# A hybrid decoder trunk in fp32: from orders written by hand to an order planned by a list scheduler

## The chip, the core and the metric

The kernel runs on one core of one Trainium2 chip. A core has TensorE (PE in the profile; PEld are its weight loads), VectorE (DVE), ScalarE (ACT), GpSimd (POOL), and SyncE (SP), whose queue issues most of the transfers. Each engine takes its instructions strictly in the order in which they are written, and waits by semaphores for what other engines or transfers have to finish first. The metric is the time of one execution in microseconds (us) on the device; of several runs the median counts.

## What is computed

Two layers of a decoder over 256 tokens with a width of 1024. A layer has a token mixer of three branches that read one projection of the normalized input, then cross-attention to 256 memory tokens, then a SwiGLU feed-forward part with an inner width of 2816.

```
for l in range(DEPTH):                                     # 2
    h = rmsnorm(x, norm_gains[l, 0])
    y = hybrid_mixer(h, ...)
    x = x + rmsnorm(y, norm_gains[l, 1])
    h = rmsnorm(x, norm_gains[l, 2]);  m = rmsnorm(mem, mem_norm[l])
    x = x + rmsnorm(cross_attention(h, m, ...), norm_gains[l, 3])
    h = rmsnorm(x, norm_gains[l, 4])
    x = x + rmsnorm(swiglu_ffn(h, ...), norm_gains[l, 5])

def hybrid_mixer(h, w_in, ...):
    z = h @ w_in
    z_q, z_kv, z_ng, z_rwkv, z_s5, z_mg = split(z)
    y_nsa  = nsa_attention(...)          # sparse attention, 8 heads of 64
    y_rwkv = rwkv7_time_mix(z_rwkv, ...) # recurrence over the tokens, 4 heads
    y_s5   = s5_layer(z_s5, ...)         # diagonal state space, 16 groups
    g_nsa, g_rwkv, g_s5 = split(sigmoid(z_mg))
    merged = g_nsa * (y_nsa @ w_up_nsa) + g_rwkv * (y_rwkv @ w_up_rwkv) + g_s5 * (y_s5 @ w_up_s5)
    return merged @ w_out
```

## The kernel before

**The main stream.** All large weights come in units of 128 x 1024 numbers, 135 a layer. SP loads a unit into `raw` (three buffers). ACT copies it, rounded, into the high part `wh` (L298), and DVE or POOL subtracts that from `raw` to get the low part `wl` (L299); of `wh` and `wl` there are four buffers each. This is called a split below. A product of two fp32 matrices is then three matmuls with these parts (`mm3`, L349 to L351): high by high, high by low, low by high. "Product" below means one of these single matmuls; a layer has 2688, and they are counted from the start of the run. In the order of the first layer: 1 to 48 the queries (512 columns wide), 49 to 288 the inputs of the RWKV and S5 branches (256 wide), 289 to 384 keys and values (48 of them 512 wide, 48 of them 280 wide), 385 to 864 most of the gates (256 wide), then to 1152 the up-projections of the three branches and the last gates, then the output projection, cross-attention and the feed-forward part.

**The small steps.** The branches RWKV (`rwkv`, stream r), S5 (`s5`, s) and sparse attention (`nsa`, n) have hundreds of small matmuls, DVE steps, ACT steps and POOL steps each. `drive` writes one step of a stream at a time, in the order of a string of letters, `MIX`, one for each layer, with m for the main stream (`mixer_main`). `XA_STEPS` does the same for cross-attention. The up-projections need the results of the branches (`yr`, `y5`, `yn`).

**What sets the order.** The order in which the code writes the instructions, moved a little by the framework's own scheduler, which knows a raised priority for a few functions (the decorator `@first`, and `HPX`): `NormT.tile`, `Post.half`, `Post.end`. The engine of each split comes from short lists, `ENGS`, which `W.engs = engs(n)` puts into force from a place on. `Weights.ahead` writes a split up to three units ahead of its products. PSUM has eight banks: three go round among the main stream's sums (`mm`), five among all else (`px`).

**Norms.** `NormT` transposes the input by token tiles (two of 128 tokens, `x` for each), splits it in high and low parts (L416 on ACT, L417 on DVE), and works out the reciprocal root of the mean square (`stat`, `rsqrt`, L366 to L381 on DVE, eight small steps in a chain), which `row` spreads along a row. `Post` scales a sub-layer's result and adds it to `x` (L444 to L458), with the same chain of small steps.

**S5 parameters.** `s5_params` makes tables from the parameters of S5 with some 170 small POOL instructions a layer on tiles of 128 x 8 (`tiny`, helpers at L465 to L500). POOL also carries splits, in the same queue.

Of the kernel before, what the change touches and what calls it, by code (L numbers as in the profile page):

```python
# [17 lines left out]
L = 2  # L18
# [9 lines left out]
# the order in which the steps of streams are written  # L28
XA_STEPS = 'kkEQ00Fv101vv0Ov1010110'
MIX = ['rmsrnmnsmrrsrmrnsmnrssnmmssmrmrrmrsnrsnnsmsnnsmrnssrmrrnmnmrsnrsnmrsnmrsrrmnmrsnmmrsnsnnrnmsmmrsnmrnrsnsmsrnrsnrmnssnrrmnsrmmssmrsssssrrmsmrsnsssnmnrrsmmsnnmsrrrrrsnrrrnmrnmnrsnmssssmrmnssnmmrnnssnnmmmsnmrrnnrmrsmsrmrsrsrsnnmsmssnnrnsnnrrmr', 'smsnmrmnrrmrssnnssmrsmmrsnsssrsrnmmrnnmrsmrnnrsnmmrsmmnmrsnrnrsnsmnrrrsmmnsmssnsrmnsnrrssnrnrsmrsnnmmnrsrmnmmrsnsrmmrrsnrrrssrmsnmsrnmmnnmsmnrrnsmnmnsnsmrsrmnrnnsrsrrnnnmmsnrsnrnnsnmsnmmmnsmrsmnsnrnnnrnrrrmnnmmsssrrrrsnmssnmmsrmrnmm']  # L30
# [5 lines left out]
TAIL = 2  # last units of weights, which have buffers of their own  # L36
MM = 3  # PSUM banks of the main stream
# [8 lines left out]
# ---------------------------------------------------------------- host layouts  # L46
# [81 lines left out]
def _mats(v):  # L128
    out = []
    for l in range(L):  # L130
# [39 lines left out]
U = 1024  # elements a partition in a unit of weights  # L170
# [61 lines left out]
# ---------------------------------------------------------------- the kernel  # L232

def body(tc, t):
    nc = tc.nc
    V, A, G, PE = nc.vector, nc.scalar, nc.gpsimd, nc.tensor

    def first(f):
        """instructions of f go before earlier ones that are ready, too"""
        def g(*a):  # L240
            with tc.high_priority(offset=HPX):
                return f(*a)
        return g

    ctx = ExitStack()
    const = ctx.enter_context(tc.tile_pool(name="const", bufs=1))
    wp = ctx.enter_context(tc.tile_pool(name="wp", bufs=2))
# [9 lines left out]
    def sb(shape, dt=F, tag=None, bufs=None):  # L257
# [9 lines left out]
        return ap.tile(list(shape), dt, tag=tag, name=nm(tag), bufs=bufs or 1)  # L267

    def ps(shape=(P, 512), tag="px", bufs=8 - MM, dt=F):
        return pp.tile(list(shape), dt, tag=tag, name=nm(tag), bufs=bufs)  # L270
# [11 lines left out]
    nc.scalar.dma_start(ident, t["consts"][:, 0:P])  # L282
# [3 lines left out]
    nc.sync.dma_start(xt[0], t["x"][0:P])  # L286
# [9 lines left out]
    # ---- weights: hi and lo parts that a product of one pass each carries  # L296
# [4 lines left out]
    class Weights:  # L301
        """the units in the order of use; loads and splits run ahead of the products"""

        def __init__(self, order):
            self.todo = order  # (layer, unit, elements)
            self.raw = []
            self.ready = []
            self.n = self.m = 0
            self.engs = [V]  # that split, in turn

        def load(self, d):
# [1334 lines left out]
```

## Time and profile before

| | before |
|---|---|
| median of 3 runs | 1130.83 us (1120.78 to 1131.45) |
| span of the profiled execution | 1125.9 us |
| granted TensorE clock, mean | 0.963 |
| PE busy, share of the span | 1037.2 us, 92% |
| DVE busy | 763.2 us, 68% |
| POOL busy | 647.3 us, 57% |
| ACT busy | 540.1 us, 48% |
| moved by DMA | 161.52 MB, 143 GB/s |

The profiled execution's own time is its span, 1125.9 us; the median of the timed runs lies 4.9 us above it. PE's busy time is a poor measure of how full it is, since matmuls overlap in its pipeline and their ends are modelled. Whether a stretch is full is seen from the number of matmuls in it.

### The profile page before, as it was taken

The page shows a single profiled execution, that of the slowest core. Times are in us where ns is not written, and L with a number is a line of the kernel's source. Part 1 is how long each engine was busy: PE and PEld are TensorE (multiplying, and loading weights), DVE is VectorE, ACT ScalarE, POOL GpSimd, SP SyncE. Part 2 cuts the span into 40 slices and gives each one's busy share as a digit, 9 for nine tenths or more (in the row PEclk, how much of TensorE's full clock was granted, in tenths as well). Part 3 has the DMA queues.
Part 4 walks back from the last instruction along what each step waited for, and adds up shares of the span by engine and source line. Part 5 has one row for each costly group of instructions (what it writes and reads, how often), then busy time and mean ns, then how long its engine had stood idle before and what let it go on. Part 6 is the DMA issues. An engine that isn't in the chain of part 4 may idle for free. (4 is left out here: it accounts for less than half of the span.)

```text
span 1125.9 us, 20473 instructions
## 1 busy us (share of the span) xinstructions
PE 1037.2 (92%) x7890; PEld 900.0 (80%) x7890; DVE 763.2 (68%) x1405; ACT 540.1 (48%) x1040; POOL 647.3 (57%) x762
## 2 busy tenths in 40 slices
PE   8887898999987999999888899999999869999997
PEld 7876676788875799998667776889788748999985
DVE  6667699898766646575458698796995764333633
ACT  7523244456555634454345242545565546444542
POOL 6999787533462586910147578964335434655543
PEclk9998999999988999999989899999899889999999
DMA  6530632244541446555434236223245314655552
GB/s 233 205 122 20 224 115 76 76 155 166 180 141 57 152 159 219 186 185 189 142 100 147 67 113 225 76 93 111 84 164 189 130 56 149 203 183 184 181 192 89
DMA packets 43153, 161.52 MB, mean 143 GB/s; under 512 B 5040, under 2 KB 5168, under 8 KB 41776
## 3 DMA queue, kind: packets, MB, share of 16 engines
q1 hardware_dynamic: 41472, 155.45, 40.7%
q10 hardware_dynamic: 1584, 4.77, 1.2%
q8 instruction: 62, 1.02, 0.4%
q14 instruction: 35, 0.29, 0.1%
HBM read 159.15 MB, written 1.05 MB: 142 GB/s over the span
## 5 line engine op out<-in xcount | busy, mean ns | idle before, releaser
L299 POOL TENSOR_TENSOR wl<-raw,wh 128x1024 fp32r<-128x1024 f32 (+1 forms) x123 | 296.7, 2420 | 327.4 <-ACT wh L298 322.0
L298 ACT ACTIVATE wh<-raw 128x1024 fp32r<-128x1024 f32 (+1 forms) x268 | 282.0, 1055 | 254.5 <-PE mm L350 107.4
L349 PE MATMUL mm<-b,wh 128*128 128x256 f32 x1344 | 386.7, 288 | 2.6 <-DVE b L1274 1.3
L351 PE MATMUL mm<-b,wl 128*128 128x256 f32 x1344 | 386.0, 288 | 1.0 <-DVE wl L299 1.0
L350 PE MATMUL mm<-b,wh 128*128 128x256 f32 x1344 | 384.4, 286 | 0.2 <-DVE b L945 0.2
L299 DVE TENSOR_TENSOR wl<-raw,wh 128x1024 fp32r<-128x1024 f32 (+1 forms) x145 | 196.7, 1357 | 166.8 <-ACT wh L298 166.6
L349 PEld LDWEIGHTS mm<-b,wh 128*128 128x128 f32 x1344 | 256.8, 191 | 12.0 <-issue 4.0
L351 PEld LDWEIGHTS mm<-b,wl 128*128 128x128 f32 x1344 | 256.6, 191 | 9.0 <-issue 6.7
L350 PEld LDWEIGHTS mm<-b,wh 128*128 128x128 f32 x1344 | 256.9, 191 | 5.7 <-issue 4.7
L350 PE MATMUL px<-wl,b 128*128 128x512 f32 x248 | 98.0, 399 | 0.0
L349 PE MATMUL px<-wh,b 128*128 128x512 f32 x248 | 97.0, 401 | 1.0 <-ACT b L298 1.0
L351 PE MATMUL px<-wh,b 128*128 128x512 f32 x248 | 97.2, 400 | 0.0
L349 PE MATMUL mm<-wh,b 128*128 128x512 f32 (+2 forms) x192 | 71.8, 382 | 13.0 <-ACT b L416 8.8
L351 PE MATMUL mm<-wh,b 128*128 128x512 f32 (+2 forms) x192 | 68.5, 370 | 5.5 <-DVE b L417 4.7
L350 PE MATMUL mm<-wl,b 128*128 128x512 f32 (+2 forms) x192 | 68.9, 364 | 0.5 <-DVE wl L299 0.5
L294 PE MATMUL px<-ident,b 128*128 128x128 f32 (+2 forms) x280 | 47.3, 287 | 12.8 <-DVE b L1432 6.7
L349 PEld LDWEIGHTS mm<-wh,b 128*128 128x128 f32 x192 | 39.8, 209 | 22.2 <-ACT b L416 13.4
L349 PEld LDWEIGHTS px<-wh,b 128*128 128x128 f32 x248 | 47.3, 191 | 11.9 <-ACT b L298 1.4
L351 PEld LDWEIGHTS px<-wh,b 128*128 128x128 f32 x248 | 47.1, 190 | 11.2
L350 PEld LDWEIGHTS px<-wl,b 128*128 128x128 f32 x248 | 47.2, 190 | 11.0
L416 ACT ACTIVATE b<-px,cols 128x128 fp32r<-128x128 f32 x128 | 41.1, 366 | 30.1 <-DVE b L417 17.2
L1568 POOL TENSOR_TENSOR b<-b,b 128x256 f32<-128x256 f32 x40 | 39.5, 989 | 26.8 <-ACT b L1567 26.7
(348 smaller groups left out, 1735.7 us busy)
## 6 DMA issues: line engine op xcount, KB each, us to landing
raw<-in_w SPq DMA_DIRECT2D x264, 512.0 KB, 3.5
b<-in_w SPq DMA_DIRECT2D x8, 1024.0 KB, 5.2
b<-in_gains ACTq DMA_DIRECT2D x6, 512.0 KB, 4.1
raw<-in_w SPq DMA_DIRECT2D x6, 420.0 KB, 3.1
b<-in_mem SPq DMA_DIRECT2D x4, 512.0 KB, 5.0
mats<-in_mats SPq DMA_DIRECT2D x1, 1152.0 KB, 7.6
mats<-in_mats ACTq DMA_DIRECT2D x1, 1152.0 KB, 6.8
x<-in_x SPq DMA_DIRECT2D x2, 512.0 KB, 5.3
```

The lines of the kernel that those rows point to most:

```text
L294: PE.transpose(out, in_, ident[:k, :k])
L298: A.activation(dst_h, src, AF.Copy)
L299: eng.tensor_tensor(dst_l, src, dst_h.bitcast(F), op=OP.subtract)
L349: PE.matmul(out, lh, rh, start=start, stop=False)
L350: PE.matmul(out, lh, rl, start=False, stop=False)
L351: PE.matmul(out, ll, rh, start=False, stop=stop)
L416: A.activation(self.h[:, n, sl], pt[:, kk], AF.Copy, scale=g[:, n:n + 1])
L1568: G.tensor_tensor(s_, s_, tg[:, 1], op=OP.mult)
```

## The change

The body is no longer written as it is run through. `Eng` stands for each engine and only notes every call in a list (`Rec.ops`), with the stream that it belongs to; each of the products of `mm3` is marked as part of one chain. `analyse` works out from the tiles which instruction needs which. `plan` then places the instructions, engine by engine, in the time of a model: of those that are ready, the one with the longest remaining path goes first. The durations come from a table in the kernel (`_cost`). The chain keeps its recorded order; other PE instructions are offered 150 ns late (`MARGIN`); streams may not run more than 30 places ahead of their oldest open step where nothing holds them (`NEAR`). `plan` picks the PSUM bank of every tile, within the three and five banks as before, and DVE or POOL for every split, whichever comes free for it first. The result is written as it is planned, with the framework's scheduler switched off. `ENGS`, the raised priorities and the run-ahead of `Weights` are without effect or gone. One letter of the first `MIX` stands four places earlier; the 2 MB of weights of the compression (`w1`, L1092) come in four loads of 512 KB for each of keys and values, not two of 1 MB; and the last steps of a layer (`finish`) are recorded ahead of the next layer's first weights.

```diff
+PE_LAT = 172
+MARGIN = 150
+DMA_LAT, DMA_NS = 1800, 0.0042
+W_SLOTS = {"raw": 3, "wh": 4, "wl": 4}
+NEAR = 30
+HORIZON = 60000.0
...
+def _cost(op, eng, out, ins, psum):
...
+    if eng == "V":
+        fast = what in ("tensor_scalar", "tensor_copy") and not inp and n >= 512
+        t = n / (1.92 if fast else 0.96) + 70
+        return t, t + 85
...
+    t = n * (2.28 if what != "tensor_scalar" else 1.7) + 100
...
+def plan(rec, info=None):
...
+    lvl = [0.0] * n
+    for i in range(n - 1, -1, -1):
+        occ, lat = min(info[i]["costs"].values())
...
+        b = occ
+        for j, kind in succ[i] + extra.get(i, []):
+            b = max(b, lvl[j] + ((lat + SEM) if kind else occ) * al)
+        lvl[i] = b
...
+    def offer(i, r):
+        for e in ops[i][0]:
+            rr = r + (MARGIN if e == "PE" and not ops[i][5] else 0)
+            heapq.heappush(pend[e], (rr, i))
+            heapq.heappush(ev, (max(rr, free[e]), e))
...
         def get(self):
-            self.ahead(1)
-            w = self.ready.pop(0)
-            self.ahead(AHEAD + max(0, min(TAIL, self.m + TAIL - len(self.todo))))
-            self.load(RAWS)
-            return w
+            l, u, k = self.todo[self.n]
+            self.n += 1
+            was, rec.stream = rec.stream, "w"
+            raw = sb([P, U], F, "raw", W_SLOTS["raw"])
+            SP.dma_start(raw[:, :k], t["w"][l, u, :, :k])
+            h, lo = sb([P, U], R, "wh", W_SLOTS["wh"]), sb([P, U], R, "wl", W_SLOTS["wl"])
+            rec.either = ("A",)
+            A.activation(h[:, :k], raw[:, :k], AF.Copy)
+            rec.either = ("V", "G")
+            V.tensor_tensor(lo[:, :k], raw[:, :k], h[:, :k].bitcast(F), op=OP.subtract)
...
     def mm3(out, lh, ll, rh, rl, start, stop):
+        rec.chain = True
         PE.matmul(out, lh, rh, start=start, stop=False)
         PE.matmul(out, lh, rl, start=False, stop=False)
         PE.matmul(out, ll, rh, start=False, stop=stop)
+        rec.chain = False
...
-        @first
         def tile(self, i, x):
...
+    with tc.manual_schedule():
+        for i, e in planned[0]:
+            _, what, a, k, _, _ = rec.ops[i]
+            getattr(real[e], what)(*a, **k)
```

In the changed kernel every instruction is written by the last line of this loop, L1988, and all PSUM tiles are called `bank`. PE and ACT have as many instructions as before; 41 splits go from DVE to POOL, so that 165 of 270 run there, where 124 did.

**The start, ACT's queue.** The place is the first norm and the first split; `x_81` and `x_82` are the token tiles of before, `x_74` and `x_75` those of the changed kernel, `b_9_95` and `b_5_79` the transposed high parts, `row_118` the row of both tiles' roots. Before:

```order
ACT_TABLE_LOAD
ACTIVATE b_35_166,tiny_165<-x_81 128x1024
ACTIVATE wh_97<-raw_88 128x1024
ACTIVATE b_9_95<-px_139,cols_85 128x128
ACTIVATE b_9_95<-px_152,cols_85 128x128
```

The changed kernel:

```order
ACT_TABLE_LOAD
ACTIVATE wh_82<-raw_81 128x1024
ACTIVATE wh_85<-raw_84 128x1024
ACTIVATE b_20_94,tiny_93<-x_74 128x1024
ACTIVATE wh_88<-raw_87 128x1024
ACTIVATE b_30_104,tiny_103<-x_75 128x1024
ACTIVATE row_118<-bank_70 128x256
ACTIVATE b_5_79<-bank_68,cols_77 128x128
```

The first transposed part, which the first product needs, stood right behind the first tile and the first split, and now stands behind both tiles and the row. In SP's queue the two tiles are loaded first and fourth before, and third and fifth now.

**POOL's queue in the first layer.** The place is the first split that POOL has among the inputs of the branches; the `tiny` tiles around it belong to the S5 parameters, `CC` is a table of theirs. Before, `wl_440` is the unit:

```order
TENSOR_TENSOR tiny_419<-tiny_416,tiny_398 128x8
TENSOR_SCALAR tiny_422<-tiny_390 128x8
TENSOR_SCALAR tiny_419<-tiny_419 128x8
TENSOR_SCALAR tiny_422<-tiny_422 128x8
TENSOR_TENSOR tiny_423<-tiny_390,tiny_422 128x8
TENSOR_TENSOR wl_440<-raw_131,wh_439 128x1024
TENSOR_SCALAR tiny_422<-tiny_422 128x8
TENSOR_SCALAR tiny_423<-tiny_423 128x8
```

The changed kernel, where `wl_249` is the eleventh unit of the run:

```order
TENSOR_TENSOR tiny_204<-tiny_204,tiny_202 128x8
TENSOR_TENSOR tiny_205<-tiny_205,tiny_202 128x8
TENSOR_TENSOR CC_221<-mats_78,tiny_204 128x256
TENSOR_TENSOR b_148_222<-mats_78,tiny_205 128x256
TENSOR_TENSOR b_149_223<-mats_78,tiny_204 128x256
TENSOR_TENSOR CC_221<-CC_221,b_148_222 128x256
TENSOR_TENSOR b_193_267<-b_41_115,cst 128x512
TENSOR_TENSOR b_148_222<-mats_78,tiny_205 128x256
TENSOR_TENSOR wl_249<-raw_247,wh_248 128x1024
```

Before, the split stood in the middle of the S5 parameters; now it stands behind nearly all of them, as POOL's 159th instruction: ahead of it are 145 that touch `tiny`, 3 splits and 10 others. Its first product is the 228th.

**PE's queue among the branches of the first layer.** The rows with 64x32, 32x256 and 128x256 x2 are small matmuls of RWKV (L677, L687), sparse attention and S5. Before, `wh_1518` and `wh_1619` are units of the gates:

```order
MATMUL mm_1816<-b_9_95,wh_1518 128x256
MATMUL mm_1816<-b_10_96,wh_1518 128x256
MATMUL mm_1816<-b_9_95,wl_1519 128x256
MATMUL px_1473<-b_350_1487,b_347_1477 32x256 x8
MATMUL px_1544<-b_225_927,b_222_906 64x32 x16
MATMUL px_1566<-b_66_300,mats_87 128x256
MATMUL px_1567<-b_66_300,mats_87 128x256
MATMUL px_1566<-b_66_300,mats_87 128x256
MATMUL px_1567<-b_66_300,mats_87 128x256
MATMUL mm_1971<-b_9_95,wh_1619 128x256
MATMUL mm_1971<-b_10_96,wh_1619 128x256
MATMUL mm_1971<-b_9_95,wl_1620 128x256
```

The changed kernel, behind product 864, the last that needs no branch:

```order
MATMUL bank_68<-b_189_263,b_234_308 64x32 x16
MATMUL bank_68<-b_256_330,cst 128x512
MATMUL bank_70<-b_188_262,b_187_261 64x32 x16
MATMUL bank_71<-b_251_325,b_235_309 64x64 x2
MATMUL bank_68<-ident,b_261_335 128x128
MATMUL bank_68<-ident,b_266_340 128x128
MATMUL bank_68<-b_249_323,CC_221 32x256 x2
MATMUL bank_68<-b_250_324,CC_221 32x256
MATMUL bank_70<-b_189_263,b_255_329 64x32 x16
MATMUL bank_68<-b_250_324,CC_221 32x256
MATMUL bank_70<-b_286_360,b_283_357 32x256 x2
MATMUL bank_69<-b_188_262,b_187_261 64x32 x16
```

Before, steps of the branches stand between products of the gates; now 864 products stand ahead, with 141 small matmuls among them, and most of the branches' steps follow with no product between them. On DVE 144 instructions, 27 of them splits, stand ahead of the last split that these products need, of 458 that DVE ran up to product 1152 in the kernel before. In the second layer it is 134, with 29 splits.

## Rows read from the trace of the kernel before

**Rows 1.** The page: busy us, share of the span, instructions; POOL's splits (busy, mean ns, idle).

```profile
PE 1037.2 (92%) x7890; PEld 900.0 (80%) x7890; DVE 763.2 (68%) x1405; ACT 540.1 (48%) x1040; POOL 647.3 (57%) x762
...
L299 POOL TENSOR_TENSOR wl<-raw,wh 128x1024 fp32r<-128x1024 f32 (+1 forms) x123 | 296.7, 2420 | 327.4 <-ACT wh L298 322.0
```

**Rows 2.** Windows: stretch, length, busy (x instructions) of PE, PEld, DVE, ACT, POOL, clock, DMA.

```profile
500.00:550.00 50.00, 50.00 (x216) 40.30 (x215) 28.09 (x28) 23.12 (x26) 0.45 (x1) 1.00 0.56 187
1000.00:1050.00 50.00, 50.00 (x424) 50.00 (x423) 17.69 (x18) 21.87 (x27) 27.77 (x18) 1.00 0.56 184
```

**Rows 3.** The same view, stretches of the two mixers.

```profile
20.90:237.80 216.90, 195.12 (x1814) 163.01 (x1813) 169.14 (x289) 92.10 (x195) 172.83 (x274) 0.96 0.37 127
...
558.80:574.40 15.60, 6.80 (x26) 4.69 (x25) 15.19 (x25) 6.88 (x17) 8.75 (x4) 0.77 0.36 111
...
150.00:300.00 150.00, 143.91 (x1187) 120.85 (x1184) 137.81 (x283) 78.33 (x193) 81.01 (x68) 1.00 0.35 118
...
0.00:292.20 292.20, 265.38 (x2309) 222.97 (x2310) 232.55 (x458) 140.97 (x308) 205.64 (x323) 0.97 0.41 140
558.80:850.30 291.50, 266.30 (x2294) 224.11 (x2293) 237.59 (x458) 138.45 (x308) 181.11 (x157) 0.95 0.35 119
```

**Rows 4.** Windows of L349 alone, one of three products: PE busy, PEld busy, clock.

```profile
0.00:20.90 20.90, 6.37 (x17) 3.20 (x17) 1.00 0.71 251
20.90:237.80 216.90, 83.52 (x272) 53.37 (x272) 0.96 0.37 127
```

**Rows 5.** Windows of DVE's splits alone (tile wl): DVE busy, clock.

```profile
0.00:292.20 292.20, 45.21 (x33) 0.97 0.41 140
558.80:850.30 291.50, 28.01 (x20) 0.95 0.35 119
```

**Rows 6.** Timeline, the start: start us, us, engine, line, operation [idle before].

```profile
4.60 1.06 ACT L422 ACTIVATE b<-x 128x1024 f32<-128x1024 f32 x1 [1.18 <-DMA x<-in_x]
...
5.79 0.15 DVE L386 TENSOR_SCALAR tiny<-tiny 128x1 f32<-128x1 f32 x1 [4.77 <-ACT b L422]
...
6.80 0.22 DVE L366 SCALAR_TENSOR_TENSOR tiny<-tiny,tiny 128x1 f32<-128x1 f32 x1
7.00 0.20 POOL L477 TENSOR_SCALAR tiny<-tiny 128x8 f32<-128x8 f32 x1
7.06 0.61 ACT L416 ACTIVATE b<-px,cols 128x128 fp32r<-128x128 f32 x2
7.19 1.23 DVE L299 TENSOR_TENSOR wl<-raw,wh 128x1024 fp32r<-128x1024 f32 x1 [0.17 <-ACT wh L298]
...
7.46 0.50 PE L349 MATMUL mm<-wh,b 128*128 128x512 f32 x1 [1.58 <-ACT b L416]
...
9.30 1.05 ACT L422 ACTIVATE b<-x 128x1024 f32<-128x1024 f32 x1
```

**Rows 7.** Windows of POOL's instructions that touch tiny: POOL busy, clock.

```profile
0.00:60.00 60.00, 35.42 (x104) 0.97 0.60 214
60.00:116.80 56.80, 17.70 (x59) 0.88 0.22 72
```

**Rows 8.** Timeline, from the first feed-forward part to the second mixer.

```profile
558.23 6.97 POOL L299 TENSOR_TENSOR wl<-raw,wh 128x1024 fp32r<-128x1024 f32 x3 [57.78 <-ACT wh L298]
...
558.38 2.24 DVE L379 SCALAR_TENSOR_TENSOR tiny<-tiny,tiny 128x1 f32<-128x1 f32 x1
...
560.65 2.26 DVE L366 SCALAR_TENSOR_TENSOR tiny<-tiny,tiny 128x1 f32<-128x1 f32 x1
...
562.94 2.27 DVE L381 SCALAR_TENSOR_TENSOR tiny<-tiny,tiny 128x1 f32<-128x1 f32 x1
```

**Rows 9.** The list of groups, DVE: operation, count, busy us, mean ns, idle before.

```profile
L299 DVE TENSOR_TENSOR wl<-raw,wh 128x1024 fp32r<-128x1024 f32 (+1 forms) x145 | 196.7, 1357 | 166.8 <-ACT wh L298 166.6
...
L366 DVE SCALAR_TENSOR_TENSOR tiny<-tiny,tiny 128x1 f32<-128x1 f32 x56 | 26.4, 472 | 1.4
```

**Rows 10.** One line of DVE: ns of one, least, median and most, first and last start.

```profile
L366 DVE SCALAR_TENSOR_TENSOR tiny<-tiny,tiny x56: 207/219/2308, 6.2 to 1120.9; 128x1 f32<-128x1 f32 x56
```

More of the change, by code (lines that the diff above doesn't have):

```diff
@@ new lines, with __init__, __getattr__, call @@
+HORIZON = 60000.0
+class Eng:
+    def __init__(self, rec, name):
+        self.rec, self.name = rec, name
+    def __getattr__(self, what):
+        def call(*a, **k):
+            r = self.rec
+            r.ops.append((r.either or (self.name,), what, a, k, r.stream, r.chain))
+        return call
+class Rec:
+    def __init__(self):
+        self.ops = []
+        self.stream = "M"
+        self.either = None
+        self.chain = False
+        self.tag = {}
+        self.caps = {}
+        self.psum = {}
+        self.np = 0
@@ new lines, in _count, with _region, _operands @@
+def _count(steps):
+    n = 1
+    for _, c in steps:
+        n *= c
+    return n
+def _region(x):
+    t = x.tensor
+    fs = 1
+    for n in t.shape[1:]:
+        fs *= n
+    steps = x.ap
+    lo = x.offset % fs
+    p0 = x.offset // fs
+    return t.name, p0, p0 + steps[0][1], lo, lo + 1 + sum((n - 1) * abs(st) for st, n in steps[1:])
+def _operands(op):
+    isap = lambda x: hasattr(x, "tensor") and hasattr(x, "ap")
+    out, ins = [], []
+    for i, x in enumerate(op[2]):
+        if isap(x):
+            (out if i == 0 else ins).append(x)
+    for key, x in op[3].items():
+        if isap(x):
+            (out if key in ("out", "accum_out") else ins).append(x)
+    return out, ins
@@ new lines, in analyse @@
+def analyse(rec):
+    hist, groups = {}, []
+    info = []
+    ops, psum = rec.ops, rec.psum
+    for i, op in enumerate(ops):
+        out, ins = _operands(op)
+        pe = op[0][0] == "PE"
+        group = op[1] == "matmul" and not (op[3]["start"] and op[3]["stop"])
+        groups.append(group)
+        preds = {}
+        acc = [(_region(x), True) for x in out if not _dram(x)] + [(_region(x), False) for x in ins if not _dram(x)]
+        for (nm, p0, p1, lo, hi), w in acc:
+            whole = nm in psum
+            for (j, q0, q1, l, u, w2, e2) in hist.setdefault(nm, []):
+                if whole and not (pe and e2):
+                    if w or w2 or ops[j][0] != op[0]:
+                        preds[j] = 1
+                elif whole and (group or groups[j]) and p0 < q1 and q0 < p1:
+                    preds.setdefault(j, 0)
+                elif (w or w2) and p0 < q1 and q0 < p1 and lo < u and l < hi:
+                    preds[j] = max(preds.get(j, 0), 0 if pe and e2 else 1)
+        for (nm, p0, p1, lo, hi), w in acc:
+            h = hist[nm]
+            if w and nm not in psum:
+                h[:] = [x for x in h if not (p0 <= x[1] and x[2] <= p1 and lo <= x[3] and x[4] <= hi and x[0] != i)]
+            h.append((i, p0, p1, lo, hi, w, pe))
+        preds.pop(i, None)
+        fn = None
+        if op[1] == "activation":
+            fn = SETS.get(str(op[2][2]).split(".")[-1])
+        info.append(dict(
+            preds=preds, fn=fn, frees=any(r[0] in psum for r, w in acc if not w), tiles=sorted({r[0] for r, _ in acc if r[0] in rec.tag}),
+            bytes=sum(4 * _count(x.ap) for x in (out + ins)[:1]) if op[1] == "dma_start" else 0,
+            costs={e: _cost(op, e, out, ins, psum) for e in op[0]}))
+    chain = [i for i in range(len(ops)) if ops[i][5]]
+    for x, y in zip(chain, chain[1:]):
+        info[y]["preds"].setdefault(x, 0)
+    return info
@@ L348, in mm3 @@
     def mm3(out, lh, ll, rh, rl, start, stop):
+        rec.chain = True
         PE.matmul(out, lh, rh, start=start, stop=False)
@@ L513, in load_mats @@
     def load_mats(l, m):
-        return (nc.scalar if l else nc.sync).dma_start(m["all"], t["mats"][l])
+        return (A if l else SP).dma_start(m["all"], t["mats"][l])
     def rwkv(st, c, m):
@@ L1473, in body @@
     for l in range(L):
-        w = [x_ for u in range(4) for x_ in W.rows(2, 512)]
         if l > 0:
             finish()
+        w = [x_ for u in range(4) for x_ in W.rows(2, 512)]
         enter(nT, 0)
```

358 lines of the change are left out of this document (287 added, 71 removed).

## The prediction

> **What bounds the kernel now.** I read the windows first, since PE's 92% [rows 1] says little: its matmuls overlap. Where PE is truly full, the number of matmuls shows it. In the feed-forward parts it is 424 matmuls of 256 columns in 50 us, or 0.118 us each, and 216 of 512 columns, or 0.231 us each, with PE busy for all 50 us [rows 2]. No order can gain there; these stretches (some 160 us in either layer) stay as they are. What is left is the two mixers.
>
> In the first mixer the stretch from 20.9 to 237.8 us holds 272 first matmuls of a triple and 17 stand before it [rows 4]: product 864, the last that needs no branch, ends at 237.8. 816 products at 0.118 to 0.231 us are some 105 us of 217. The rest is small matmuls and waiting for what feeds them. The reader should see in [rows 3] that no engine is full there: DVE has 169 of 217 us, POOL 173. Up to 292.2 us, where by the same count product 1152 ends, DVE has 232.6 us in 458 instructions and POOL 205.6. DVE is nearest to a bound; its best rate in a long stretch is 137.8 of 150 us, or 0.92 [rows 3]. The second mixer is alike: 237.6 us of DVE in 291.5 us.
>
> **The change part by part: the order.** The code that PE, ACT and DVE run is the same; what moves is when. In the changed order the first 864 products come early, with 141 small matmuls between them, and the branches' steps come behind. So each mixer falls in two: a first stretch paced by PE, and a second paced by DVE, whose queue holds what was not done in the first. I sum the first layer so.
>
> Start: the first product needs `b_5`, which now stands on ACT behind the row of both tiles. Tiles and units arrive at a spacing of (9.30 - 4.60)/3 = 1.57 us, since before the second tile's square, at 9.30, was three loads behind the first's, at 4.60 [rows 6]. Now the second tile is the fifth load, four spacings behind 4.60, so 10.9 us. Then the square and its accumulator 1.06 + 0.2, the eight steps of the root (six stand from 5.79 to 7.02, so 1.6), two steps of 0.4 for the row, and one eviction 0.3: the first product starts at 14.9 us, not at 7.46. Behind it the 48 products of the queries run unhindered, 48 x 0.231 = 11.1, to 26.0 us. Before, this took to 20.9: a loss of 5 us, unless PE makes it good where it waits later.
>
> Products 49 to 864: 720 of 256 columns, 85.0 us; 48 of 512, 11.1; 48 of 280 at 0.13, 6.2; small matmuls between them some 8 us by my estimate (123 at under 0.07 us). That would be 110 us if nothing holds PE.
>
> One thing does. The eleventh unit's split is on POOL behind 145 instructions on `tiny`. Such an instruction takes (35.42 + 17.70)/163 = 0.326 us on average [rows 7], and 0.20 us undisturbed [rows 6]. The third unit, fourth load, lands at 9.3 us; ACT's copy (1.06) and POOL's split (2.42, [rows 1]) bring POOL to 12.8. Behind that come the 145 tiny ones (47.3 us, or 29.7 undisturbed; none is taken as done earlier), two more splits, its own the last, and ten others at some 0.5 by my estimate. The eleventh unit is ready at 70 us by the mean and at 52 by the least. PE is there (product 228) at 26.0 + 180 x 0.118 + 2 = 49 us. So PE waits 3 to 21 us; I take the middle, 13, because the mean includes POOL's waits for DVE, which has less to do beside them now. The products behind and the two DVE splits in the ring are held as well. Product 864 then ends at 26.0 + 110.3 + 13 = 149 us, against 237.8.
>
> That is no gain by itself, because DVE's work is still to be done. In its first 144 instructions DVE has 27 splits of 1.36 us [rows 9] and 117 others. These cost (232.55 - 45.21)/(458 - 33) = 0.44 us each [rows 3, 5], so 36.8 + 51.7 = 88.5 us of 149. The remaining 232.6 - 88.5 = 144.1 us come behind it. At 0.92, the best rate that the trace shows, this is 156.6 us, and product 1152 ends at 306 us, not at 292.2: **+14 us**. I take the best rate and not that of the whole stretch (169.1/216.9 = 0.78), because the queue is now sorted by the length of the path behind each step.
>
> **The second layer.** From the end of the feed-forward part at 558.8 us the next mixer's products flow at 574.4 [rows 3]. These 15.6 us are DVE's chain of a norm: three of its small steps take 2.24, 2.26 and 2.27 us beside POOL's three splits of 6.97 us [rows 8], and 0.22 us is what such a step takes alone [rows 6, 10]. Four of the next units' splits were on POOL, two are now, so I take off two such steps, 4 us, and have 11.6. Then 11.1 for the queries and 110.3 as above, but no wait for POOL, since the second layer's parameters are made earlier: 133 us. DVE had 20 splits in this mixer [rows 5], and has 32 now. With 434 others, 32 x 1.36 + 434 x 0.442 = 235.4 us. Its first 134 instructions, 29 of them splits, are 86 us. The rest, 149.4/0.92 = 162.4, ends at 295.5 us, against 291.5: **+4 us**.
>
> **Cross-attention and feed-forward.** Four norms end there by the same chain. The splits beside those of cross-attention were all on POOL and are now mixed; I take off one step of 2 us a layer, **-4 us**. In the feed-forward part most splits of the last weights go to POOL. A unit's 12 products last 12 x 0.231 = 2.77 us and POOL's split 2.42 [rows 1, 2], so this is hidden as long as POOL does nothing else. If it weren't, 15 such units would cost some 5 us a layer. The four smaller loads of `w1` move the same bytes, and lie among 0.37 of DMA use [rows 3]; nothing for them. PSUM banks are as many as before.
>
> Sum: 1125.9 + 14 + 4 - 4 = 1140 us of span; the median lies 4.9 us above the profiled span, so **1145 us**, 1.2% slower.
>
> **Rivals.** First, *faster*: DVE's work shrinks. Before, POOL's work and DVE's lie beside each other for all of the mixer. Now POOL has done most of its 205.6 us in the first stretch; about 56 us of it are left for the second by the order. L366's mean is 472 ns against a median of 219, 14 us over 56 of them [rows 9, 10]; DVE's splits take 1357 against 1230 ns, 18 us [rows 6, 9]. With the other steps of those chains I estimate 40 us in all, 20 a layer. If the second stretch is spared these, the first layer ends at 149.3 + 124.1/0.92 = 284.2 (-8), the second at 133.1 + 129.4/0.92 = 273.8 (-18), and the norms lose no steps, -8: 1125.9 - 34 + 4.9 = **1097 us**. For it speaks that the long steps stand exactly beside POOL's splits [rows 8]; against it, that the median of L366 is undisturbed already, so that few steps meet a split.
>
> The Trainium skill, in "SBUF — State Buffer", section "🔬 SBUF: two separate sides", says why such steps grow: VectorE and GpSimd share one pair of ports as an exclusive lock, and whoever starts first holds it for the whole instruction. The 2.24 us beside a split of some 2.3 agree with it. By that page alone, any sorting of POOL's work away from DVE's would pay, which is the 1097 us above; the page says nothing of how often they meet.
>
> Second, *slower still*: the second stretch is bound by the chains between engines, not by DVE's queue. RWKV's steps go from PE to DVE to ACT and back; with no products between them PE idles, and DVE with it. The rate is then the 0.78 of the whole mixer [rows 3]: 144.1/0.78 gives +42 in the first layer, 149.4/0.78 gives +33 in the second, together 1125.9 + 75 - 4 + 4.9 = **1202 us**. PE that idles also loses its clock, as from 558.8 to 574.4 us, where it was busy 6.8 of 15.6 us at a granted 0.77 [rows 3]. It decides wherever the branches' steps, alone, keep DVE less than 0.87 busy.
>
> Third, *no change, since the order only trades*: PE waits the 3 us for POOL, not 13, and DVE runs at 0.95. The first layer then ends at 139.3 + 151.7 = 291 (-1), the second at 133.1 + 157.3 = 290.4 (-1), the norms as above: 1125.9 - 6 + 4.9 = **1125 us**. That the plan doesn't do what it says belongs here: its table gives a small POOL instruction of 8 columns some 118 ns, against 0.326 us [rows 7]. A plan that is wrong on the engine that holds PE up spends in waits what it wins by its sorting.
>
> **How the numbers follow.** About 1% is what a measurement of this kernel can tell from no change. The forecast has 0.30, the slower rival 0.14, no change 0.24, the faster one 0.32, since its mechanism is in the rows and its size is open. So faster by over 1% 0.32, within 1% 0.24, slower by over 1% 0.44. The range has to reach from the faster rival nearly to the slower one: 1088 to 1196 us. The forecast's own range is 1132 to 1165: the wait for POOL 3 to 21 us, and DVE's rate 0.95 to 0.87.
>
> **What would show it.** In the changed profile: the first product at 14 to 16 us; PE idle before product 228 at about 49 us for a split on POOL; product 864 near 149 us, with DVE under 0.65 busy until then; then DVE at 0.9 or more up to product 1152, near 306 us. The steps of a norm's chain at 2.2 us would be fewer. If DVE is below 0.85 there and waits for PE or ACT, the second rival holds. If its splits and small steps are shorter by 10% or more, the first does. I would be wrong in kind if product 864 comes much later than 165 us: then something other than POOL holds the products, such as the four buffers of split weights or the evictions behind the gates.

## The result, and the profile after

The changed kernel takes 1255.65 us (median; 1253.47 to 1260.41) against 1129.42 us in the same rounds: a ratio of 1.1124, 95% interval 1.1068 to 1.1179. It is 11% slower. The forecast was 1145 us and 1088 to 1196: the direction was right, the size far off.

The page of the changed kernel: busy time, granted TensorE clock in 40 slices, and the splits on POOL and DVE. They answer to [rows 1, 9].

```profile
PE 1113.9 (89%) x7890; PEld 938.3 (75%) x7890; DVE 651.1 (52%) x1364; ACT 542.6 (43%) x1040; POOL 745.5 (60%) x803
...
PEclk9899986998898999999999798659799989999999
...
L1988 POOL TENSOR_TENSOR wl<-raw,wh 128x1024 fp32r<-128x1024 f32 x165 | 398.4, 2417 | 326.2 <-ACT wh L1988 301.1
...
L1988 DVE TENSOR_TENSOR wl<-raw,wh 128x1024 fp32r<-128x1024 f32 (+1 forms) x105 | 151.6, 1447 | 139.4 <-ACT wh L1988 134.7
```

DVE has 112 us less to do than before (763.2 [rows 1]); 45 of them are less time in splits, since POOL took some over. So DVE did not become the bound. The clock line shows where to look: each digit is a slice of 31 us; a 6 stands in the first mixer, and 8, 6, 5 in the second.

The trace lets one count products (matmuls that read `wh` or `wl`) on PE. Their start times in us, worked out from both traces:

```
product        before   after        before   after
           (first layer)          (second layer)
   1            7.5    16.5         567.7    613.2
  48           20.9    29.1         585.2    631.5
 228           51.0    66.1         615.0    658.4
 384          109.7   102.1         672.4    682.9
 864          237.8   174.8         792.0    774.9
 900          248.5   270.0         805.1    907.1
1152          292.2   343.9         850.3    971.9
1500          387.0   439.2         947.0   1067.2
```

Nearly all of the loss arises in the mixers. It is 51.7 us at product 1152 of the first layer and 52.2 at product 1500; in the second layer it grows from 45.5 us at product 1 to 121.6 at product 1152, and stays at 120.2 up to product 1500. Between the two mixers 6.7 us are won back, and the last feed-forward part adds 5.5. The products do run ahead as forecast (864 is 63 us early), and then comes a gap of 95 us in the first layer and 132 in the second in which almost no product is issued.

The windows of those gaps, of the rest up to product 1152, and of the two mixers as a whole (columns as in [rows 3]):

```profile
174.80:270.00 95.20, 77.38 (x725) 47.08 (x724) 64.73 (x138) 18.32 (x42) 41.69 (x54) 0.80 0.18 60
270.00:303.60 33.60, 31.40 (x239) 28.01 (x238) 25.75 (x76) 14.90 (x45) 11.84 (x10) 0.95 0.32 110
303.60:343.90 40.30, 36.94 (x228) 26.03 (x227) 30.16 (x91) 22.63 (x65) 7.25 (x4) 0.83 0.25 79
...
774.90:907.00 132.10, 107.92 (x939) 68.95 (x938) 81.42 (x187) 23.45 (x65) 50.85 (x70) 0.70 0.12 41
907.00:937.40 30.40, 26.24 (x205) 23.35 (x203) 22.55 (x52) 13.57 (x37) 17.75 (x12) 1.00 0.32 105
937.40:971.90 34.50, 31.45 (x216) 22.77 (x216) 28.39 (x81) 20.57 (x59) 7.15 (x3) 0.95 0.30 107
...
0.00:343.90 343.90, 296.66 (x2301) 240.45 (x2302) 209.82 (x447) 139.55 (x299) 207.40 (x325) 0.90 0.34 115
612.90:971.90 359.00, 305.15 (x2281) 243.73 (x2280) 212.64 (x450) 134.89 (x297) 202.89 (x316) 0.84 0.30 100
```

In the gaps PE is the busiest engine (77 of 95 us, 108 of 132), with 725 and 939 matmul records, all but some 37 of them small, at a granted clock of 0.80 and 0.70. DVE is at 0.68 and 0.62, far from the 0.92 of the forecast.

A second count says what the gap costs. For every run of small matmuls between two products, take the time from its first matmul to the next product, waits included. Between product 49 and 1152 this sums, over some 1112 to 1120 records (an fp32 matmul leaves two or more), to:

```
                small matmuls, us    longest run, records / us    granted clock there
                first    second      first         second         first  second
before           97.6     96.4       228 / 17.7     80 / 7.3       0.97   0.98
after           152.6    165.6       658 / 84.5    902 / 125.0     0.83   0.76
```

The differences, 55 and 69 us, are together about what the mixers lose from product 48 on (43 and 75 us). The same matmuls, in nearly the same number, take 1.6 and 1.7 times as long when most of them stand in one heap.

### The profile page after: what moved, and what is told of

Its sections match the earlier page's. It is cut to its first block, busy times and chain, and to the rows that moved or that the text cites. A ratio compares the mean times of both kernels' runs of the same rounds, so it can differ in the third digit from the quotient of the medians.

```text
span 1251.6 us, 20503 instructions
## 1 busy us (share of the span) xinstructions
PE 1113.9 (89%) x7890; PEld 938.3 (75%) x7890; DVE 651.1 (52%) x1364; ACT 542.6 (43%) x1040; POOL 745.5 (60%) x803
## 5 line engine op out<-in xcount | busy, mean ns | idle before, releaser
L1988 POOL TENSOR_TENSOR wl<-raw,wh 128x1024 fp32r<-128x1024 f32 x165 | 398.4, 2417 | 326.2 <-ACT wh L1988 301.1
L1988 PE MATMUL bank<-b,wh 128*128 128x256 f32 x2688 | 517.3, 293 | 35.6 <-DVE b L1988 9.8
L1988 PEld LDWEIGHTS bank<-b,wh 128*128 128x128 f32 x2688 | 437.4, 199 | 45.3 <-DVE b L1988 11.9
L1988 PE MATMUL bank<-b,wl 128*128 128x256 f32 x1344 | 391.4, 291 | 9.4 <-POOL wl L1988 8.5
L1988 ACT ACTIVATE wh<-raw 128x1024 fp32r<-128x1024 f32 (+1 forms) x270 | 284.0, 1054 | 255.4 <-PE bank L1988 152.7
L1988 PE MATMUL bank<-wh,b 128*128 128x512 f32 (+2 forms) x896 | 271.1, 380 | 17.9 <-ACT b L1988 12.8
L1988 PEld LDWEIGHTS bank<-b,wl 128*128 128x128 f32 x1344 | 267.0, 199 | 12.2 <-POOL wl L1988 9.1
L1988 DVE TENSOR_TENSOR wl<-raw,wh 128x1024 fp32r<-128x1024 f32 (+1 forms) x105 | 151.6, 1447 | 139.4 <-ACT wh L1988 134.7
L1988 POOL TENSOR_TENSOR b<-b,b 128x256 f32<-128x256 f32 (+2 forms) x200 | 173.4, 891 | 77.3 <-DVE b L1988 46.8
L1988 PEld LDWEIGHTS bank<-wh,b 128*128 128x128 f32 x896 | 165.9, 192 | 57.6 <-ACT b L1988 20.0
L1988 PE MATMUL bank<-b,b 64*64 64x32 f32 (+10 forms) x1696 | 164.2, 303 | 24.9 <-DVE b L1988 19.0
L1988 PE MATMUL bank<-wl,b 128*128 128x512 f32 (+2 forms) x448 | 169.5, 378 | 8.1 <-POOL wl L1988 7.3
L1988 PEld LDWEIGHTS bank<-b,b 64*64 64x64 f32 (+5 forms) x1696 | 104.5, 170 | 86.9 <-DVE b L1988 36.6
L1988 ACT ACTIVATE b<-bank 128x512 f32<-128x512 f32 (+9 forms) x158 | 72.5, 468 | 213.7 <-PE bank L1988 176.3
L1988 PEld LDWEIGHTS bank<-wl,b 128*128 128x128 f32 x448 | 86.3, 193 | 25.4 <-POOL wl L1988 11.8
L1988 DVE TENSOR_TENSOR b<-bank,row 128x512 f32<-128x512 f32 (+1 forms) x60 | 35.8, 599 | 110.8 <-PE bank L1988 110.3
L1988 DVE TENSOR_SCALAR tiny<-tiny 128x1 f32<-128x1 f32 (+5 forms) x114 | 19.5, 179 | 114.9 <-ACT b L1988 113.5
L1988 DVE TENSOR_TENSOR b<-bank,b 128x512 f32<-128x512 f32 (+3 forms) x102 | 56.3, 566 | 20.9 <-PE bank L1988 15.3
L1988 ACT ACTIVATE b<-b 128x256 f32<-128x256 f32 (+5 forms) x88 | 43.7, 514 | 52.7 <-POOL b L1988 36.1
L1988 PE MATMUL bank<-ident,b 128*128 128x128 f32 (+3 forms) x344 | 54.7, 300 | 12.5 <-DVE b L1988 7.1
L1988 PEld LDWEIGHTS bank<-ident,b 128*128 128x128 f32 (+3 forms) x344 | 35.6, 149 | 30.7 <-DVE b L1988 11.3
L1988 ACT ACTIVATE b<-bank,cols 128x128 fp32r<-128x128 f32 x128 | 41.3, 374 | 26.9 <-DVE b L1988 20.0
```

Of the source, the lines that this page charges most:

```text
L1988: getattr(real[e], what)(*a, **k)
```

## The experiments

Five theories were on trial. **A (heap):** the planner ranks by the longest remaining path alone. In its own reckoning the first RWKV matmul lies 34.5 us of path ahead of product 865, the first of S5 15.1, the first of sparse attention 11.5 *behind* it, and the 480 gate products 56.6. So it holds the branches back until few gates are left, without regard to the PE time that the first layer's 661 small steps still need, and they pile up. **B (splits):** the 41 splits that went to POOL. **C (start):** the late first product and POOL's queue of S5 parameters. **D (clock):** the lower clock in the heap. **E (price):** the table's 0.118 us for a POOL instruction that takes 0.326 [rows 7].

**Weight on the branches.**

```diff
-ALPHA = {}
+ALPHA = {"r": 6.0, "s": 6.0, "n": 6.0}
```

> Theory A (pile-up): the planner ranks by longest remaining path and not by how much work still has to pass an engine, so the branches' small matmuls fall behind all 864 products and then stand alone on PE (0.111 us each instead of 0.081, and 17 us more of idle PE, in the first mixer). This kernel counts latencies in the three branch streams six-fold in that ranking; 563 of the first layer's 661 small PE steps then stand ahead of product 864, where the changed kernel has 132. By A the two mixers lose their extra 52 and 67 us, and the run takes 1105 to 1160 us. Theory B (the splits moved from DVE to POOL) and theory C (the late start and the waits for POOL behind the S5 parameters): none of that changes here, so 1235 to 1265 us.

Measured: 1199.23 us, ratio 1.0636 (1.0603 to 1.0669), 56 us less than the changed kernel, between the ranges that A and its rivals gave. Small matmuls take 134.1 and 116.1 us, in heaps of at most 132 and 272 records. B and C are out as the main cause, since the edit touches neither: POOL has 170 splits (165 in the changed kernel), and the first product comes at 16.7 us (16.5). A has the right sign and not the whole size.

**The recorded order.**

```diff
         lvl[i] = b
+    lvl = [10.0 * (n - i) for i in range(n)]
```

> The same planner, but what is ready goes by the place in the recorded program (the hand-written order of steps) and not by the longest remaining path. By theory A (pile-up) that alone brings the branches' steps back between the products (653 of 661 ahead of product 864) and the time to 1105 to 1170 us. By theories B and C it stays at 1235 to 1265 us, since splits still go to POOL (100 on DVE) and the POOL queue is as long.

Measured: 1226.15 us, 1.0875 (1.0843 to 1.0907), again between the two ranges. The sum hides two answers, which the windows from product 48 to 1152 of the first and the second layer show, of the kernel before, of the changed kernel and of this run:

```profile
20.90:292.20 271.30, 248.09 (x2225) 209.20 (x2224) 219.88 (x414) 126.76 (x279) 193.94 (x288) 0.97 0.38 131
585.20:850.30 265.10, 248.70 (x2228) 210.68 (x2227) 217.60 (x404) 124.19 (x277) 170.02 (x153) 0.97 0.36 123
...
29.10:343.90 314.80, 274.95 (x2217) 222.07 (x2216) 196.12 (x405) 122.30 (x266) 188.85 (x261) 0.89 0.32 107
631.50:971.90 340.40, 289.40 (x2219) 232.27 (x2218) 195.53 (x405) 121.54 (x269) 195.53 (x311) 0.84 0.29 99
...
28.10:356.90 328.80, 286.31 (x2217) 229.66 (x2216) 193.47 (x397) 126.47 (x274) 221.71 (x380) 0.83 0.31 101
669.50:936.80 267.30, 251.61 (x2220) 207.20 (x2219) 180.77 (x388) 119.95 (x265) 154.45 (x125) 0.98 0.37 120
```

The second mixer takes 267.3 us; before it is 265.1 and in the changed kernel 340.4. Here the ranking alone gives back 73 of the 75 us, at a clock of 0.98. The first takes 328.8 us, at 0.83. What it has and the second hasn't is POOL's work on S5 parameters: POOL is busy 221.7 us there and 154.5 in the second, and 60.6 and 0.1 of these us are instructions on `tiny`. The recorded order also makes cross-attention worse: 117.3 and 107.3 us from product 1152 to 1500, where the path ranking has 95.2.

**The splits as before.**

```diff
+PICK = "VVVVVVVVGVVG...
...
-            rec.either = ("V", "G")
+            rec.either = (PICK[self.n - 1],)
```

> The engine of every split is that of the kernel before, given by a string; order and banks are planned as in the changed kernel. Theory B (picks): 1130 to 1190 us. Theory A (pile-up): 100 of 661 small steps stand ahead of product 864, as badly as in the changed kernel, so 1230 to 1270 us.

Measured: 1241.7 us, 1.1013 (1.0981 to 1.1045). The heaps stay (798 and 519 records, 108.0 and 93.1 us), and the time falls by 14 us: the first mixer is 13 us longer (327.8), the second 20 shorter (320.7). B falls as the main cause. What the splits are worth by themselves this doesn't say, since the plan around them moved as well.

**The start.** Loads and ACT's first steps are tied to the order of before:

```diff
+    for x, y in head_order(rec):
+        info[y]["preds"].setdefault(x, 0)
...
+    return [(xs[0], raws[0]), (raws[1], xs[1]), (xs[1], raws[2]), (ev[3], sq[1])] + [(i, row) for i in ev]
```

> Only the start is put right: the token tiles are loaded first and fourth, and ACT writes the transposed parts ahead of the row. Theory C (start) as I predicted it: the first product comes at 8 to 10 us and not at 16.5, and what is won there goes through to the end, since product 864 follows in a row: 1238 to 1248 us. Theory A agrees on the sign and gives no more than these 8 us; if the run is unchanged within 3 us, the start was hidden behind a later wait.

Measured: 1266.46 us, 1.1232 (1.1166 to 1.1299). This expectation missed on the other side. The first product comes at 11.3 us, 5.2 earlier, but product 228, behind POOL's S5 parameters, at 66.0, as before the edit (66.1). Product 864 comes at 169.3, 5.5 earlier. Then the planner answers with a larger heap (833 records, 101.8 us, where it was 658), and product 1152 comes at 357.0, 13 later. An edit to a planned kernel changes more than its place, so this run doesn't price the start. The last experiment comes nearer to that.

**Recorded order, with a better price.**

```diff
-    t = n * (2.28 if what != "tensor_scalar" else 1.7) + 100
+    t = n * (2.28 if what != "tensor_scalar" else 1.7) + 300
...
+    lvl = [10.0 * (n - i) for i in range(n)]
```

> Recorded order again (as in the run with that order alone, 1226 us), and the planner's price of a POOL instruction 0.2 us higher, near what the profile shows for the small ones (0.326 against the table's 0.118). Then the planner gives 131 splits to DVE instead of 100 and puts 128 instead of 208 POOL instructions ahead of product 288. Theory A with E (in the first layer the wrong price of POOL's S5 steps loads POOL with splits early, PE waits, and the first mixer takes 329 us where the second takes 267): the first mixer falls to 270 to 295 us, the run to 1130 to 1180. If the price doesn't matter: 1215 to 1235 us.

Measured: 1181.68 us, 1.043 (1.0385 to 1.0475), just above the range. The windows of the same two stretches as above:

```profile
28.00:303.00 275.00, 261.84 (x2217) 211.67 (x2216) 202.71 (x416) 129.65 (x277) 206.22 (x418) 0.96 0.37 121
601.90:889.30 287.40, 270.60 (x2220) 219.80 (x2218) 183.21 (x387) 120.42 (x266) 147.94 (x123) 0.90 0.34 111
```

The first mixer falls from 328.8 to 275.0 us (before: 271.3), with 7 splits on POOL in it where 26 had been. So E is a cause of its own under the recorded order. Between them these two runs bring each mixer back to within 4 us of before, with nothing but another ranking and one number; no single run does it for both.

The second mixer, though, is 20 us slower than in the run above, with nearly the same order on PE. They issue at the same pace from product 408 to 432 and, but for 2 us, from 456 to 612; from 432 to 456 the one takes 27.6 us and the other 39.0. (The other half of the 20 us is lost before product 408, at a granted 0.89 against 0.97.) The windows of products 432 to 444 and 444 to 456, first of the run with recorded order alone:

```profile
781.10:800.00 18.90, 16.90 (x154) 10.85 (x153) 16.05 (x34) 7.08 (x20) 9.49 (x9) 1.00 0.09 29
800.00:808.70 8.70, 8.70 (x77) 5.89 (x77) 6.20 (x29) 2.09 (x8) 2.94 (x3) 1.00 0.01 2
```

and of the run with the price:

```profile
724.40:751.60 27.20, 25.30 (x155) 16.35 (x153) 15.61 (x33) 6.96 (x20) 9.26 (x9) 0.67 0.06 20
751.60:763.40 11.80, 11.80 (x78) 7.56 (x77) 6.50 (x27) 1.65 (x7) 2.97 (x3) 0.61 0.00 1
```

Nearly the same matmuls, DVE, ACT and POOL about equally busy, and PE idle for 2 us in either: what differs is the granted clock, 1.00 against 0.67 and 0.61. Rows of the timeline say it for single groups, first at the full clock, then at the lower one; the first row of each is the last wait of PE ahead of them:

```profile
787.44 0.29 PE L1989 MATMUL bank<-b,mats 128*64 128x16 f32 x4 [1.45 <-DVE b L1989]
...
792.60 1.13 PE L1989 MATMUL bank<-b,mats 32*128 32x256 f32 x6
793.66 1.97 PE L1989 MATMUL bank<-tiny,b 128*128 128x32 f32 x16
```

```profile
730.78 0.29 PE L1989 MATMUL bank<-b,mats 128*64 128x16 f32 x4 [1.78 <-DVE b L1989]
...
738.89 2.07 PE L1989 MATMUL bank<-b,mats 32*128 32x256 f32 x6
740.90 3.62 PE L1989 MATMUL bank<-tiny,b 128*128 128x32 f32 x16
```

This pair shows D: the clock by itself is worth 11.4 us in these 39.

**The price alone**, in the changed kernel.

> The changed kernel with only the planner's price of a POOL instruction raised by 0.2 us. Small PE steps ahead of product 864: 48 of 661, so the pile-up is as before. Theory A: 1235 to 1265 us, however well the splits are chosen. Theory E (the wrong price of POOL is the cause by itself): 1130 to 1190 us.

Measured: 1229.07 us, 1.0848 (1.0797 to 1.09), a little below A's range. The heap is larger than ever (901 records, 137.3 us, in the first layer), and the time falls by 27 us only: the second mixer is 35 us shorter (305.5), the first 13 longer (328.0). The price by itself doesn't remove the heap.

**Four banks, and a filler in the heap.**

```diff
-    slots["px"] = [(0.0, b) for b in range(MM, 8)]
+    slots["px"] = [(0.0, b) for b in range(MM, 7)]
```

> The changed kernel with four instead of five PSUM banks for all that isn't the main stream; the eighth bank is empty. It is the control of the next run. 1245 to 1275 us by all theories; clearly more if the branches are short of banks.

Measured: 1280.22 us, 1.13 (1.1264 to 1.1335), above the range: one bank less, with the plan made anew for it, costs some 20 to 25 us. Then, in the two heaps:

```diff
+                if not rec.ops[i][5] and (at - WARM) % 2688 in range(864, 901):
+                    small += 1
+                    if small % 3 == 0:
+                        nc.tensor.matmul(banks[7][:, :P], wz, wz, start=True, stop=True)
```

> As the run with four banks, and behind every third small PE step of the two pile-ups a matmul of zeros by zeros, 128 x 128, into the empty bank: some 290 in all, 0.11 us each at full clock, so 32 us of added PE work, with no result used. Theory D (much of the loss is that TensorE is granted the lower clock while the small steps stand alone, 0.80 and 0.70 on average): the granted clock in the pile-ups rises to 0.9 or more, the small steps get shorter, and the run takes no longer than its control, or up to 30 us less. If the clock isn't what counts, or stays where it was: 15 to 35 us more than the control.

Measured: 1457.42 us, 1.2864 (1.2643 to 1.3085), 177 us above its control, against every theory. The heaps of the control, then those with the filler:

```profile
181.20:285.90 104.70, 84.79 (x762) 51.97 (x761) 69.10 (x166) 21.36 (x58) 41.73 (x54) 0.77 0.17 54
795.40:921.00 125.60, 98.98 (x944) 65.95 (x943) 86.55 (x203) 24.91 (x72) 51.85 (x72) 0.73 0.14 43
```

```profile
178.70:346.10 167.40, 156.95 (x1017) 103.72 (x1016) 66.61 (x166) 21.48 (x58) 40.56 (x54) 0.82 0.11 35
855.00:1106.60 251.60, 234.65 (x1267) 153.20 (x1266) 85.11 (x203) 25.13 (x72) 51.58 (x72) 0.63 0.07 22
```

The clock didn't rise for good (0.77 to 0.82, and 0.73 to 0.63), so the run can't test D. It says something else: 288 matmuls were added, and the two stretches grew by 63 and 126 us, with PE busy for 72 and 136 us more. Work added on PE in the heap is paid nearly in full. And one such matmul between small ones takes much more than 0.11 us, even where the clock is full (granted 1.00 from 220 to 240 us):

```profile
230.32 0.30 PE L1989 MATMUL bank<-b,b 64*64 64x32 f32 x4
230.55 0.49 PE L1995 MATMUL bank<-wz 128*128 128x128 f32 x2
230.97 0.41 PE L1989 MATMUL bank<-b,b 64*64 64x32 f32 x6
```

From its start to the next it is 0.42 us. So the heap is bound for the most part by what PE issues itself; the waits for other engines, 20 of 105 and 27 of 126 us in the control, are the smaller part.

**Two other rankings**: a branch step ranks no lower than the product behind it in the recorded order; the first with the better price, the second with the splits of before.

```diff
+        if ops[i][5]:
+            due = lvl[i]
+        elif ops[i][4] in "rsn":
+            lvl[i] = max(lvl[i], due + 0)
```

> Ranks by longest path as the changed kernel does, but a step of a branch ranks no lower than the product that follows it in the hand-written order, and POOL is priced 0.2 us higher. Small PE steps ahead of products 384, 600 and 864: 247, 397, 505 of 661 in the first layer; in the second 193, 243 and 360 of 649, so that there a third of them are still behind. Theory A (pile-up): the first mixer 285 to 305 us, the second 295 to 320, cross-attention at the 95 us that the path ranking has, in all 1135 to 1175 us. If the pile-up weren't the cause: above 1200.

> The same ranking with the old price of POOL, and the engine of every split as in the kernel before. Ahead of products 384, 600, 864 stand 273, 581, 653 of 661 small steps in the first layer, and 193, 415, 499 of 649 in the second. Theory A with E: 1125 to 1165 us, the second mixer at 285 to 300. If it is not under 1150, order and picks of the kernel before do not make up its time, and the order inside DVE's and ACT's queues counts as well.

Measured: 1194.6 us, 1.0571 (1.0514 to 1.0629), and 1213.89 us, 1.0742 (1.0635 to 1.0848). Both are better than the changed kernel and worse than A allowed. Mixers from product 48 to 1152: 290.7 and 294.8, 303.1 and 306.6 us, at clocks of 0.89 to 0.92; small matmuls 127 to 131 us. In the second layer heaps of 390 and 332 records are left, but in the first, where none is over 95 records, the time isn't back either. By the expectation of the second run, the orders inside DVE's and ACT's queues may then count as well.

**The pieces together**: recorded order between products 49 and 1152 of a layer, longest path elsewhere, the better price; then the same with the start put right.

```diff
+        for i in range(prods[o + 1151], prods[o + 48] - 1, -1):
+            due = max(due, lvl[i]) if ops[i][5] else due
+            lvl[i] = due + 0.001 * (n - i)
...
```

> Recorded order for everything recorded between product 49 and product 1152 of a layer (and for what that needs), longest path elsewhere, POOL priced 0.2 us higher. This puts together what the earlier runs showed one by one: the first mixer from product 48 to 1152 in 275 us (recorded order with the price), the second in 267 (recorded order) or 287 (where the clock fell), cross-attention in 95 and not the 105 of recorded order, 19 us from the last product of the first layer to product 48 of the second. Theory A with E, pieces added up: 1135 to 1165 us, depending on whether the lower clock is met. Above 1185: the pieces do not add up.

> The run before, and the start put right as in the run of the start alone (token tiles first and fourth, transposed parts ahead of the row). All orders behind it are nearly the same, so that this is the clean test of the start: if it counts as I predicted, 4 to 8 us less than the run before; if it is hidden behind a later wait (POOL's S5 steps), within 2 us of it.

Measured: 1174.95 us, 1.0383 (1.0297 to 1.0468), and 1174.06 us, 1.0394 (1.0329 to 1.0459). The best of the planned versions, and slower than before; the first is 10 us above its range. Its cross-attention is back at 95.7 and 96.1 us, as the pieces said. Its mixers are not, and the first should have been 275:

```profile
30.30:327.30 297.00, 274.76 (x2225) 220.42 (x2224) 208.62 (x424) 128.76 (x282) 178.95 (x259) 0.91 0.34 113
616.20:903.80 287.60, 269.55 (x2228) 219.36 (x2227) 194.99 (x420) 124.72 (x278) 182.68 (x231) 0.91 0.36 117
```

The second of the two was made to price the start, since nearly all behind it is the same: the first product comes at 11.4 us instead of 16.7, product 228 at 56.0 instead of 59.2, product 384 at 111.5 instead of 112.1. So what the start wins is gone by product 384. The medians differ by 0.9 us, but with executions that spread over 15 and 10 us they couldn't tell 5 us by themselves. Nor do the two profiles agree behind product 384: product 1152 comes at 327.3 and 317.5 us, with a granted 0.87 against 0.91 from product 384 to 864.

## Why the prediction was wrong

**What held.** The order was read rightly: the products run ahead and the branches' steps stand behind them in a heap. The start costs what was said or a little more (first product 16.5 us, not 14.9; product 48 at 29.1, not 26.0), but in the last two runs it was gone by product 384, so its 5 us should have been no term of the sum. PE does wait for POOL's splits, for 5.6 and 2.9 us where 13 were put down:

```profile
35.28 0.58 PE L1988 MATMUL bank<-b,wl 128*128 128x256 f32 x1 [5.56 <-POOL wl L1988]
...
64.33 0.39 PE L1988 MATMUL bank<-b,wl 128*128 128x256 f32 x1 [2.89 <-POOL wl L1988]
```

The transition to the second mixer got shorter, from 26.5 to 18.6 us up to product 48; 4 were forecast. Cross-attention took 95.2 us in either layer, against 94.8 and 96.7 before, so the 2 us a layer did not come. The feed-forward parts, put at no change, took 2 and 5.5 us longer.

**The step that failed** is "a second paced by DVE", with "the best rate and not that of the whole stretch". The second stretch was given as 156.6 and 162.4 us; it took 169.1 and 197.0. DVE had 120.6 and 132.4 us of work in it, not 144 and 149, so the forecast was wrong twice over, in opposite directions: less work, at a rate of 0.71 and 0.67. That the sign came out right is luck. The wrong term is PE's. It was costed for the products, and the small matmuls were put down as "some 8 us" in the first stretch and not costed at all in the second, since DVE seemed the bound. They take 97.6 us in the first mixer of before, interleaved, and 152.6 in the changed one, mostly in a heap. The windows of before [rows 3] had them: 1814 matmuls in 216.9 us, of which 816 were products. The runs with another ranking show that their place is the main cause (73 us of the second mixer came back by it alone), and the pair at two clocks shows one reason why.

**The first stretch** was also too short in the forecast: 146 us from product 48 to 864, not 123. The wait for POOL was smaller than said, so it isn't that; small matmuls and short waits between products, at a clock of 0.94, are what is left to fill it. This part was not taken apart further.

**The rivals.** "Slower still" named the right place and half of the reason. Its mark, DVE below 0.85 there and waiting for PE, is what the profile shows, and so is the clock. Its price was too low (1202 us), because it took the rate of a stretch in which products and small steps were mixed. The "faster" rival's mechanism is half there: DVE's work up to product 1152 went from 232.6 to 209.8 us in the first layer. Its splits did not get shorter (45.2 us for 33 of them before, 44.9 for 31 after), so it's the other steps that did, from 0.44 to 0.40 us on average. That agrees with the Trainium skill, "SBUF — State Buffer", "🔬 SBUF: two separate sides", on the lock that DVE and POOL share; no run here tests the lock by itself. It doesn't show in the time, since the second stretch isn't paced by DVE.

**How much is the clock.** With half of the speed at the lower level, a granted 0.80 means that 40% of the 95.2 us, and 0.70 that 60% of the 132.1 us, ran at 1.2 GHz. Applied to PE's busy time there (77.4 and 107.9 us) and halved, this is 15 and 32 us, some 48 of the 119 us that the mixers lost: an estimate, not a measurement. The rest is the heap itself, and the traces show that it is there at the full clock too. By their clock records, between product 864 and 865 the clock was full for 50.4 of 84.6 us in the first layer and for 51.1 of 126.5 in the second. In these full-clock stretches PE started 389 and 410 records, one in 130 and 125 ns; interleaved, before, it was one in 87 (97.6 us over 1120). The mix of shapes isn't quite the same, and what fills these 40 ns was not taken apart. The Trainium skill, "TensorE: Matmul & The Clock Gate", "HAM oscillation — how this bites in real kernels", says that a long enough wait between bursts puts PE back to the lower clock, so that each burst starts slow. The rows agree that the clock is lower where PE idles: 0.77 from 558.8 to 574.4 us in the kernel before, with PE busy for 6.8 of 15.6 us [rows 3]. They show more than that: from 751.6 to 763.4 us, in the run with recorded order and price, PE was busy for all of 11.8 us at a granted 0.61. PE's last wait before was 1.78 us, up to 730.78; at the same place in the run with the order alone it was 1.45 us, and the clock stayed full.

**What stays open.** Why the last versions keep 20 to 25 us in a mixer, though their small matmuls stand in heaps of at most 70 records. They run at 0.91 and 0.92, where the mixers of before have 0.97; reckoned as above, a difference of 0.06 over some 290 us makes 16 us, an estimate again. The executions of one of them spread from 1168 to 1183 us, at mean clocks of 0.942 to 0.932. What makes the clock fall at a given place was not found. Nor were the orders inside DVE's and ACT's queues tested by themselves.

## What to carry to other kernels

A list scheduler that ranks by the longest remaining path doesn't see how much work must still pass one engine; a hundred microseconds of small matmuls with a path of 35 are started too late. When work is to be spread, rank it by when it must begin given the load of its engine, or keep a hand-written order as the rank. The first of these wasn't tried here, and with the second the best planned version was still 4% slower than the order written by hand. And before a moved step is called free, count what every engine has to issue in the stretch that it moves to, PE's small matmuls too: their price is that of the new neighbourhood, not of the old.

## What the runs showed of the hardware

The granted clock can stay at the lower level while PE has no idle time in the profile (a mean of 0.61 over 11.8 us, with PE busy for all of them), and it acts on small matmuls nearly in full: 2.07 against 1.13 us and 3.62 against 1.97 us for the same groups. Two programs with almost the same order met different clocks at the same place, and one lost 11.4 us in 39 there. A 128 x 128 fp32 matmul between 64 x 32 ones took 0.42 us from its start to the next one's at the full clock, where 0.11 had been reckoned. At the full clock a record of the small matmuls took 125 to 130 ns in a heap, and 87 ns between products at 0.97.
